# Layer boundary of a hybrid trunk: two-part dt weights, statistics in the z banks, an earlier stick-breaking chain and a fixed engine order

## The chip, the cores and the metric

One core of one Trainium2 chip. The metric is device microseconds (us) of one execution; the kernel before has a median over three runs, and one further execution was profiled.

## The reference, cut to what matters

Two post-norm residual layers over T = 272 tokens (16 learned meta tokens and 256 frames) with model width 2048. Layer 0 is four heads of gated linear attention and eight heads of stick-breaking attention behind one input and one output projection; layer 1 is a Mamba-2 mixer with 8 groups of 8 heads. After each layer comes a layer norm over `ALPHA * h + f`. All is float32.

```python
for layer in range(2):
    f = even_mixer(h, ...) if layer == 0 else odd_mixer(h, ...)
    h = layer_norm(ALPHA * h + f, ln_g[layer], ln_b[layer])

def layer_norm(x, g, b):
    xc = x - mean(x);  return xc * rsqrt(mean(xc * xc) + LN_EPS) * g + b

def odd_mixer(h, ...):
    z, xbc, dt_raw = split(h @ w_in)                # dt_raw has 64 columns
    xbc = silu(causal_conv(xbc));  xs, bs, cs = split(xbc)
    dt  = softplus(dt_raw + dt_bias)
    y   = ssd(xs, bs, cs, dt, a_log, d_skip)        # decays: exp of cumulated dt * a
    return rms_norm_groups(y * silu(z)) @ w_out
```

## The kernel before

Activations lie transposed: 16 blocks (`KT`) of 128 features by 272 tokens. Weights come from memory as "units" of 128 x 2048 f32, layer 0's units first (`L0`), then layer 1's (`L1`); tile `raw` has three buffers. Each half of a unit is split into a high and a low part (`whi` by ScalarE at L146, `wlo` mostly by VectorE at L147), each part tile with five buffers. One product is three matmuls (`three`, L165 to L167): whi by xhi, whi by xlo, wlo by xhi. An input unit is 16 blocks, so 48 matmuls into one PSUM tile `pj` (four buffers); `po` has two buffers, and two "z banks" are held apart. Side work (attention chains, convolutions, norms) are generators that `tick` steps between quarters of a unit. A list scheduler then decides the order of each engine, except where code pins it.

The place of the change is the boundary of the two layers. The last units of layer 0 are four `out0c` units (`u[2]` = 4 to 7): each adds two blocks to `hacc` (L462), after which `stat0` writes the scaled block as `xhi` (ScalarE, L815) and `xlo` (VectorE, L816), and has squares and sums for the norm gathered (ScalarE L836, GpSimd L834 and L837); the last two blocks go to TensorE unsummed (`spare`). `norm0` runs the 64 columns of the dt projection as 16 x 3 matmuls on the un-normalised blocks, then sums over features by matmuls with a matrix of ones (mean: L848, L852; squares: L849, L853), and works out mean and 1/std (L858 to L868, `newton` L253 to L255); both end in the z banks as `mean_p` and `rs_p`.

Layer 1's first six units (`NFIRST`; B, C, z and three x) also run on un-normalised blocks with two more columns, and `fix` (L899 to L902) corrects their results with mean and 1/std. Meanwhile `normalize0` centres (L927), scales (L928) and shifts (ScalarE) `hacc` block by block; then the normalised blocks are split again (`xhi` by ScalarE, `xlo` by VectorE, L920 and L921) for the seventh unit, an x unit, on. `residual1` transposes the normalised `hacc` into `acc` (L942, L943). `dt_path` makes softplus (L956 to L969) and three scans (L976), sends the sums to memory (`edr`), and transposes them on TensorE (L984, L986). `load_decay` reads `edr` back broadcast over the partitions (`ebc`), from which `decay1` makes the matrices `M` (L1047, L1048, exponential, product at L1074) that group 0's output matmuls (L1172) need.

A stick-breaking head has three units, q, k and v; `mix_sb` is its chain of scores, weights and values (values at L590), whose result `mixh` and `mixl` feed the output units.

## Time and profile before

| what | value |
|---|---|
| median of three runs | 1404.34 us (1403.64 to 1405.53) |
| the profiled execution | 1404.02 us |
| its span in the trace | 1402.3 us |
| TensorE busy | 1382.8 us, 99% of the span |
| VectorE busy | 1024.5 us, 73% |
| ScalarE busy | 769.0 us, 55% |
| GpSimd busy | 324.2 us, 23% |

The time of an execution is some 1.7 us more than the span between the first and the last instruction of the trace. Matmuls are pipelined: one of 272 columns is shown as 0.29 us long, while the next starts 0.125 us after it, so lengths of TensorE are read from start to start. A float32 matmul (not split) is recorded in two halves, so x2 stands for one of them. PE is TensorE, PEld its weight loads, DVE VectorE, ACT ScalarE, POOL GpSimd, SP the engine that issues the transfers.

### The profile page before, as it was taken

The page shows a single profiled execution, that of the slowest core. Times are in us where ns is not written, and L with a number is a line of the kernel's source. Part 1 is how long each engine was busy: PE and PEld are TensorE (multiplying, and loading weights), DVE is VectorE, ACT ScalarE, POOL GpSimd, SP SyncE. Part 2 cuts the span into 40 slices and gives each one's busy share as a digit, 9 for nine tenths or more (in the row PEclk, how much of TensorE's full clock was granted, in tenths as well). Part 3 has the DMA queues.
Part 4 walks back from the last instruction along what each step waited for, and adds up shares of the span by engine and source line. Part 5 has one row for each costly group of instructions (what it writes and reads, how often), then busy time and mean ns, then how long its engine had stood idle before and what let it go on. Part 6 is the DMA issues. An engine that isn't in the chain of part 4 may idle for free.

```text
span 1402.3 us, 26080 instructions
## 1 busy us (share of the span) xinstructions
PE 1382.8 (99%) x10701; PEld 1329.7 (95%) x10701; DVE 1024.5 (73%) x1663; ACT 769.0 (55%) x1138; POOL 324.2 (23%) x285
## 2 busy tenths in 40 slices
PE   9999999999999999999999999999999999999996
PEld 8999999999999999999999899899898999989985
DVE  7857575575565675558799989777887768778687
ACT  6645454364345544545587766555555565565651
POOL 0000110100101100114402325342332433424323
PEclk9999999999999999999999999999999999999998
DMA  9544444445444445444444755655556456454651
GB/s 326 183 153 165 168 155 176 165 167 172 159 172 160 151 154 192 156 155 142 151 151 172 265 175 192 213 192 178 207 175 227 154 192 218 161 204 149 222 196 61
DMA packets 37720, 249.84 MB, mean 178 GB/s; under 512 B 4256, under 2 KB 6112, under 8 KB 9184
## 3 DMA queue, kind: packets, MB, share of 16 engines
q1 hardware_dynamic: 37168, 247.77, 50.7%
q8 instruction: 84, 1.38, 0.4%
q10 hardware_dynamic: 432, 0.39, 0.1%
q14 instruction: 36, 0.29, 0.1%
HBM read 245.94 MB, written 2.20 MB: 177 GB/s over the span
## 4 chain that ended last, share of the span: by engine, by line
PE 83%; DVE 7%; ACT 4%; issue 2%; POOL 2%; DMA 1%; ACTq 0%; SPq 0%; POOLq 0%; DVEq 0%
PE pj L166 21%; PE pj L165 21%; PE pj L167 21%; PE pj L476 4%; PE pj L477 4%; PE pj L478 4%; DVE wlo L147 2%; PE po L1172 2%; ACT whi L146 1%; PE po L590 1%; DVE xlo L816 1%; POOL wlo L147 1%; DMA ebc<-edr 1%; DMA hacc<-in_xT 1%; POOL xt L1010 1%
## 5 line engine op out<-in xcount | busy, mean ns | idle before, releaser
L165 PE MATMUL pj<-xhi,whi 128*128 128x272 f32 (+4 forms) x2560 | 734.2, 287 | 1.5 <-ACT xhi L317 0.5
L166 PE MATMUL pj<-xlo,whi 128*128 128x272 f32 (+4 forms) x2560 | 731.3, 286 | 0.0
L167 PE MATMUL pj<-xhi,wlo 128*128 128x272 f32 (+4 forms) x2560 | 729.8, 285 | 0.0
L147 DVE TENSOR_TENSOR wlo<-raw,whi 128x1024 fp32r<-128x1024 f32 (+2 forms) x405 | 514.2, 1273 | 244.8 <-ACT whi L146 243.2
L146 ACT ACTIVATE whi<-raw 128x1024 fp32r<-128x1024 f32 (+2 forms) x435 | 451.1, 1038 | 396.4 <-PE pj L166 329.7
L165 PEld LDWEIGHTS pj<-xhi,whi 128*128 128x128 f32 x2560 | 481.6, 188 | 4.9 <-ACT whi L146 1.7
L166 PEld LDWEIGHTS pj<-xlo,whi 128*128 128x128 f32 x2560 | 482.6, 189 | 1.5 <-issue 0.6
L167 PEld LDWEIGHTS pj<-xhi,wlo 128*128 128x128 f32 x2560 | 482.0, 188 | 0.5 <-issue 0.4
L165 PE MATMUL pj<-mixh,whi 128*128 128x272 f32 x384 | 111.2, 291 | 1.0 <-ACT mixh L801 1.0
L167 PE MATMUL pj<-mixh,wlo 128*128 128x272 f32 x384 | 110.7, 289 | 0.0
L166 PE MATMUL pj<-mixl,whi 128*128 128x272 f32 x384 | 110.7, 289 | 0.0
L147 POOL TENSOR_TENSOR wlo<-raw,whi 128x1024 fp32r<-128x1024 f32 x30 | 75.7, 2524 | 118.7 <-ACT whi L146 118.5
L476 PE MATMUL pj<-whi,yh 128*128 128x512 f32 (+1 forms) x244 | 94.8, 388 | 0.0
L478 PE MATMUL pj<-whi,yl 128*128 128x512 f32 (+1 forms) x244 | 94.2, 386 | 0.0
L477 PE MATMUL pj<-wlo,yh 128*128 128x512 f32 (+1 forms) x244 | 94.2, 386 | 0.0
L248 POOL TENSOR_TENSOR gr<-gr,gsc 128x1088 f32<-128x1088 f32 x6 | 15.4, 2570 | 302.6 <-ACT gsc L247 302.6
L165 PEld LDWEIGHTS pj<-mixh,whi 128*128 128x128 f32 x384 | 72.2, 189 | 1.3 <-ACT mixh L801 1.1
L166 PEld LDWEIGHTS pj<-mixl,whi 128*128 128x128 f32 x384 | 72.3, 188 | 0.2
L167 PEld LDWEIGHTS pj<-mixh,wlo 128*128 128x128 f32 x384 | 72.3, 188 | 0.1
L485 DVE SCALAR_TENSOR_TENSOR acc<-pj,rr,acc 128x512 f32<-128x512 f32 (+1 forms) x65 | 46.1, 734 | 15.2 <-PE pj L478 15.1
L478 PEld LDWEIGHTS pj<-whi,yl 128*128 128x128 f32 x244 | 45.8, 188 | 9.2
L476 PEld LDWEIGHTS pj<-whi,yh 128*128 128x128 f32 x244 | 45.8, 188 | 9.1
(327 smaller groups left out, 1518.7 us busy)
## 6 DMA issues: line engine op xcount, KB each, us to landing
raw<-in_wts SPq DMA_DIRECT2D x212, 1024.0 KB, 4.8
ebc<-edr SPq DMA_DIRECT2D x8, 1664.0 KB, 6.4
raw<-in_wts SPq DMA_DIRECT2D x9, 256.0 KB, 5.7
hacc<-in_xT SPq DMA_DIRECT2D x7, 272.0 KB, 5.4
early<-in_wts SPq DMA_DIRECT2D x2, 512.0 KB, 7.1
lg<-in_lnr SPq DMA_DIRECT2D x1, 1024.0 KB, 4.5
lb<-in_lnr SPq DMA_DIRECT2D x1, 1024.0 KB, 4.5
out_h<-acc SPq DMA_DIRECT2D x2, 512.0 KB, 2.6
```

Source lines behind the costliest of these rows:

```text
L146: self.nc.scalar.activation(hi, src, AF.Copy)
L147: eng.tensor_tensor(lo, src, hi.bitcast(F32), op=ALU.subtract)
L165: mm(ps, whi, xhi, start=first, stop=False)
L166: mm(ps, whi, xlo, start=False, stop=False)
L167: mm(ps, wlo, xhi, start=False, stop=last)
L248: mul(c, c, e, op=ALU.mult)
L476: mm(ps, yh[:, kk, tt], hi[:, k, :], start=kk == 0, stop=False)
L477: mm(ps, yh[:, kk, tt], lo[:, k, :], start=False, stop=False)
L478: mm(ps, yl[:, kk, tt], hi[:, k, :], start=False, stop=kk == 3)
L485: self.nc.vector.scalar_tensor_tensor(a, ps, r[:, t : t + 1], a, op0=ALU.mult, op1=ALU.add)
L590: mm = lambda r, a, b, start=False, stop=False: self.nc.tensor.matmul(o[:, r], a, b, start=start, stop=stop, skip_group_check=True)
L1172: mm(o[i * 64 : (i + 1) * 64, jj, t0:S], xd[:, s, h * 64 : (h + 1) * 64], M[:, h, c0:c1], start=(s, jj) == (0, 0), stop=False, **gk,)
```

## The change

It has five parts.

1. The dt weights are loaded at `out0c` unit 4 and split at unit 5 (before: 6 and 7), with the 64 columns' high and low parts side by side in one 128-column tile. A block then takes two matmuls (both parts by xhi, both by xlo) instead of three; rows 64 to 127 of the result hold the low part's share, and one float32 matmul with `add2` (two identity matrices one above the other) adds the halves.
2. The statistics go to the z banks instead of `po` tiles, ahead of and between the dt matmuls, and that order is pinned.
3. A head's `mix_sb` starts after its k unit, one unit earlier, and waits for v only ahead of the values.
4. VectorE and ScalarE keep the order of the program from `out0c` unit 6 to the end of the centring.
5. The centring moves from `normalize0` into `norm0` and takes two blocks per instruction (128 x 544), the first two instructions ahead of `newton`; the scaling takes two blocks as well. The halves of layer 1's second unit are split there.

```diff
+    def keep_order(self, first):
+        ins = self.traced()
+        n0 = next(n for n in reversed(range(len(ins))) if ins[n] is first)
...
+        for eng in (mybir.EngineType.DVE, mybir.EngineType.Activation):
+            mine = [i for i in ins[n0:] if i.engine == eng]
+            for a, b in zip(mine, mine[1:]):
+                self.tc.add_manual_dep(b, a.name, free, reason="keep_order")
...
         if u[2] == 6:
-            self.dt_raw = self.lp.tile([P, 1024], F32, tag="gu", name="dtraw")
-            self.nc.sync.dma_start(self.dt_raw, self.wdt)
-        if u[2] == 7:
-            self.dt_parts = self.split(self.dt_raw, 1024)
+            self.first = self.traced()[-1]
+        if u[2] == 4:
+            self.dt_raw = self.lp.tile([P, 2, 8, 64], F32, tag="gu", name="dtraw")
+            self.nc.sync.dma_start(self.dt_raw.rearrange("p a k c -> p (a k c)"), self.wdt)
+        if u[2] == 5:
+            self.dt_parts = [self.lp.tile([P, 8, 2, 64], F32R, tag=n, name="dt" + n, bufs=2) for n in ("gvh", "gvl")]
+            for a, p in enumerate(self.dt_parts):
+                self.split_into(self.dt_raw[:, a], p[:, :, 0, :], p[:, :, 1, :], self.nc.vector)
...
     def post_sk(self, ps, h, j):
-        self.cur["k"] = self.sb_parts(ps, ("ke", "gk")[h % 2], 1.0)
+        k = self.sb_parts(ps, ("ke", "gk")[h % 2], 1.0)
+        v = self.cur["sv", h] = self.v_tiles(h)
+        self.mixers[4 + h // 4].append(self.push(self.mix_sb(h, self.cur["q"], k, v)))
...
-        yield from _wait(tv, self.tasks["sr", h // 4])
+        while ("sv", h) not in self.tasks:
+            yield
+        yield from _wait(self.tasks["sv", h], self.tasks["sr", h // 4])
...
-        hi, lo = [a.rearrange("p (k c) -> p k c", c=64) for a in self.dt_parts]
+        pin = self.tc.keep_in_program_order
+        pm, pq = self.zb
+        pin(mm(pm[:, :T], self.ones, self.ssum, start=True, stop=False))
+        pin(mm(pq[:, :T], self.ones, self.ssq, start=True, stop=False))
         for k in range(KT):
-            self.in_kt(self.ps_dt[:64, :TG], hi[:, k, :], lo[:, k, :], k, 0, TG)
-        pm, pq = self.po(), self.po()
...
+            if k == 10:
+                for n, (x, q) in enumerate(self.spare):
+                    l = n == len(self.spare) - 1
+                    pin(mm(pm[:, :T], self.ones, x, start=False, stop=l))
+                    pin(mm(pq[:, :T], self.ones, q, start=False, stop=l))
+            w = self.dt_parts[k // 8][:, k % 8].rearrange("p a c -> p (a c)")
+            pin(mm(self.ps_dt[:, :TG], w, self.xhi[:, k, :], start=k == 0, stop=False))
+            pin(mm(self.ps_dt[:, :TG], w, self.xlo[:, k, :], start=False, stop=k == KT - 1))
+        self.split_half(len(L0) + 1, 0)
...
+        def center(ks):
+            for k in ks:
+                h = self.hacc[:, k : k + 2, :]
+                vec.tensor_tensor(h, h, two(self.mean_p), op=ALU.subtract)
...
+        center((0, 2))
         self.newton(rs, var, tmp)
...
         act(self.rs_p, rs, AF.Copy)
+        self.split_half(len(L0) + 1, 1)
+        center(range(4, KT, 2))
+        self.keep_order(self.first)
...
-        self.tasks["dt"] = self.push(self.dt_path(fix(self.ps_dt, 64, 0, scr[:, 2048 : 2048 + T]), scr))
+        add2 = lp.tile([P, 64], F32, tag="add2", name="add2")
+        vec.tensor_tensor(add2, self.ident[:, :64], self.ident[:, 64:], op=ALU.add)
+        both = scr[:, 2048 + 2 * T : 2048 + 2 * T + TG]
+        act(both, self.ps_dt[:, :TG], AF.Copy)
+        ps = self.po()
+        nc.tensor.matmul(ps[:64, :TG], add2, both, start=True, stop=True)
+        self.tasks["dt"] = self.push(self.dt_path(fix(ps, 64, 0, scr[:, 2048 : 2048 + T]), scr))
...
-        for k in range(KT):
-            h = self.hacc[:, k, :]
-            nc.vector.tensor_tensor(h, h, self.mean_p, op=ALU.subtract)
-            nc.vector.tensor_tensor(h, h, self.rs_p, op=ALU.mult)
-            nc.scalar.activation(h, h, AF.Identity, bias=self.col(C_LB, k), scale=self.col(C_LG, k))
-            if k % 2:
-                yield
+        for k in range(0, KT, 2):
+            h = self.hacc[:, k : k + 2, :]
+            nc.vector.tensor_tensor(h, h, two(self.rs_p), op=ALU.mult)
...
```

The order of TensorE at the end of the dt projection, before (`po_8046` is the dt projection, `po_8095` the sum for the mean, `pj_8138` layer 1's first unit; the sums of squares, L849 and L853, stand 27 matmuls of `pj_8138` later):

```order
L165 MATMUL po_8046<-xhi,whi_7976 64x274
L166 MATMUL po_8046<-xlo,whi_7976 64x274
L167 MATMUL po_8046<-xhi,wlo_7977 64x274
L165 MATMUL po_8046<-xhi,whi_7976 64x274
L848 MATMUL po_8095<-ssum,ones 128x272
L852 MATMUL po_8095<-hacc,ones 128x272
L166 MATMUL po_8046<-xlo,whi_7976 64x274
L167 MATMUL po_8046<-xhi,wlo_7977 64x274
L852 MATMUL po_8095<-hacc,ones 128x272
```

And of the change (`z_64` and `z_65` are the z banks, `po_8048` the dt projection, `pj_8143` layer 1's first unit; ahead of this piece the two sums `ssum` and `ssq` go to the z banks right behind layer 0's last matmul, and then come the dt matmuls of ten blocks):

```order
L875 MATMUL po_8048<-xhi,dtgvl 128x274
L876 MATMUL po_8048<-xlo,dtgvl 128x274
L872 MATMUL z_64<-hacc,ones 128x272
L873 MATMUL z_65<-nsq_8029,ones 128x272
L872 MATMUL z_64<-hacc,ones 128x272
L178 MATMUL pj_8143<-xhi,whi_7982 128x274
L179 MATMUL pj_8143<-xlo,whi_7982 128x274
L180 MATMUL pj_8143<-xhi,wlo_7983 128x274
L178 MATMUL pj_8143<-xhi,whi_7982 128x274
L873 MATMUL z_65<-nsq_8046,ones 128x272
L875 MATMUL po_8048<-xhi,dtgvl 128x274
L876 MATMUL po_8048<-xlo,dtgvl 128x274
```

The last sum of squares now stands four matmuls of the first unit behind the sum for the mean, and the dt matmuls of the last six blocks come behind both.

The order of VectorE behind the variance, before (L253 to L255 is `newton`, L899 and L900 `fix`, L927 the centring):

```order
L860 SCALAR_TENSOR_TENSOR var<-po_8096,ntmp 128x272
L861 TENSOR_SCALAR var<-var 128x272
L253 TENSOR_TENSOR ntmp<-stats_8103 128x272
L254 SCALAR_TENSOR_TENSOR ntmp<-ntmp,var 128x272
L255 SCALAR_TENSOR_TENSOR stats_8103<-ntmp,stats_8103 128x272
L147 TENSOR_TENSOR wlo_8327<-raw_8230,whi_8326 128x1024
L880 MEMSET mt_8125 48x128
L881 MEMSET xd_8126 48x256
L899 COPY uv_8131<-po_8046 64x2
L899 COPY uv_8219<-pj_8138 128x2
L927 TENSOR_TENSOR hacc<-hacc,z_64 128x272 x11
```

And of the change (L266 to L268 is `newton`, L889 the centring, L160 the split):

```order
L894 SCALAR_TENSOR_TENSOR var<-z_65,ntmp 128x272
L895 TENSOR_SCALAR var<-var 128x272
L889 TENSOR_TENSOR hacc<-hacc,z_64 128x544 x2
L266 TENSOR_TENSOR ntmp<-stats_8091 128x272
L267 SCALAR_TENSOR_TENSOR ntmp<-ntmp,var 128x272
L268 SCALAR_TENSOR_TENSOR stats_8091<-ntmp,stats_8091 128x272
L915 MEMSET mt_8125 48x128
L916 MEMSET xd_8126 48x256
L945 TENSOR_TENSOR add_8131<-ident 128x64
L160 TENSOR_TENSOR wlo_8108<-raw_7978,whi_8107 128x1024
L889 TENSOR_TENSOR hacc<-hacc,z_64 128x544 x6
L160 TENSOR_TENSOR wlo_8219<-raw_8141,whi_8218 128x1024
```

Two centring instructions stand between the variance and `newton`, and the other six behind one split, ahead of every `fix`; before, all sixteen stood behind `newton`, eleven of them ahead of the first `fix` on the dt projection.

The order of TensorE where the dt sums are transposed, before (`pj_8990` is layer 1's tenth unit, a z unit, of which 16 matmuls stand ahead; L1061 to L1063 are scores of group 0, L984 and L986 the transposes):

```order
L165 MATMUL pj_8990<-xhi,whi_8912 128x256
L1061 MATMUL z_65<-bc_8225 128x256
L1062 MATMUL z_65<-bc_8225 128x144
L1063 MATMUL z_65<-bc_8225 16x16
L984 MATMUL po_8603<-ident,dt_scr 128x64
L166 MATMUL pj_8990<-xlo,whi_8912 128x256
L167 MATMUL pj_8990<-xhi,wlo_8913 128x256
L984 MATMUL po_8603<-ident,dt_scr 128x64 x3
L986 MATMUL po_8603<-ident,dt_scr 16x64 x2
```

And of the change (`pj_8796` is layer 1's eighth unit, `pj_8884` its ninth, both z units; L1027 and L1029 are the transposes):

```order
L179 MATMUL pj_8796<-xlo,whi_8756 128x256
L180 MATMUL pj_8796<-xhi,wlo_8757 128x256
L178 MATMUL pj_8884<-xhi,whi_8797 128x256
L1027 MATMUL po_8576<-ident,dt_scr 128x64
L179 MATMUL pj_8884<-xlo,whi_8797 128x256
L1027 MATMUL po_8576<-ident,dt_scr 128x64 x3
L1029 MATMUL po_8576<-ident,dt_scr 16x64 x2
L180 MATMUL pj_8884<-xhi,wlo_8798 128x256
```

The transposes stand behind one matmul of the ninth unit, where they stood behind sixteen of the tenth: 63 matmuls of 256 columns earlier in TensorE's order. Of the other places that TensorE waited at, the transposes of `residual1` (L942) have their fifth group of four 24 matmuls of the sixth unit behind the fourth group (before: two), the values of the last stick-breaking head stand 28 matmuls ahead of the first matmul that reads them (before: none), and group 0's output matmuls (L1172) stand behind 31 matmuls of the thirteenth unit (before: two). On SP the transfers of `edr` and `ebc` now follow the load of layer 1's twelfth unit directly; before, `edr` followed that of the thirteenth, and `ebc` that of the fourteenth.

## Rows read from the trace of the kernel before

**Rows 1.** The page: busy time, share of the span and instructions of each engine.

```profile
PE 1382.8 (99%) x10701; PEld 1329.7 (95%) x10701; DVE 1024.5 (73%) x1663; ACT 769.0 (55%) x1138; POOL 324.2 (23%) x285
```

**Rows 2.** What TensorE waited for over the whole span: line, what it waited for, us in total, times, longest.

```profile
PE po L1172 <- DVE M L1074: 1.8, 1, 1.8
PE po L942 <- ACT acc L943: 1.2, 1, 1.2
...
PE pj L165 <- ACT mixh L801: 1.0, 1, 1.0
```

**Rows 3.** TensorE in order of time around the last value matmul: start, us, instruction, in brackets the wait ahead of it and its releaser.

```profile
648.38 0.22 PE L590 MATMUL po<-s,v 80*128 80x16 f32 x1
649.60 0.77 PE L165 MATMUL pj<-mixh,whi 128*128 128x272 f32 x4 [0.99 <-ACT mixh L801]
```

**Rows 4.** TensorE in order of time through the dt projection, the statistics and layer 1's first unit (columns as in rows 3).

```profile
681.65 0.29 PE L165 MATMUL po<-xhi,whi 128*64 128x274 f32 x1
...
686.89 0.31 PE L165 MATMUL po<-xhi,whi 128*64 128x274 f32 x1
687.39 0.34 PE L166 MATMUL po<-xlo,whi 128*64 128x274 f32 x1 [0.20 <-DVE xlo L816]
...
688.54 0.34 PE L165 MATMUL po<-xhi,whi 128*64 128x274 f32 x1 [0.68 <-ACT xhi L815]
688.71 0.62 PE L848 MATMUL po<-ssum,ones 128*128 128x272 f32 x2
689.17 0.62 PE L852 MATMUL po<-hacc,ones 128*128 128x272 f32 x2
...
690.36 0.49 PE L165 MATMUL pj<-xhi,whi 128*128 128x274 f32 x1
...
698.02 0.28 PE L165 MATMUL pj<-xhi,whi 128*128 128x262 f32 x1
```

**Rows 5.** VectorE in order of time ahead of that wait.

```profile
684.69 1.21 DVE L147 TENSOR_TENSOR wlo<-raw,whi 128x1024 fp32r<-128x1024 f32 x1
685.82 0.77 DVE L462 TENSOR_TENSOR hacc<-hacc,pj 128x272 f32<-128x272 f32 x2
```

**Rows 6.** TensorE in order of time at the residual's transposes, layer 1's sixth and seventh units.

```profile
729.07 0.49 PE L942 MATMUL po<-ident,hacc 128*128 128x128 f32 x3
729.32 0.37 PE L166 MATMUL pj<-xlo,whi 128*128 128x274 f32 x1
729.53 0.29 PE L167 MATMUL pj<-xhi,wlo 128*128 128x274 f32 x1
731.05 0.66 PE L942 MATMUL po<-ident,hacc 128*128 128x128 f32 x4 [1.24 <-ACT acc L943]
732.03 0.40 PE L165 MATMUL pj<-xhi,whi 128*128 128x272 f32 x1 [0.32 <-DVE fix L900]
```

**Rows 7.** One stretch by engine: start:end and length, then busy us and instructions of PE, PEld, DVE, ACT and POOL, the granted clock, the DMA share, GB/s.

```profile
699.10:753.30 54.20, 52.64 (x433) 51.89 (x431) 54.03 (x122) 42.45 (x80) 1.43 (x1) 1.00 0.41 144
```

**Rows 8.** Groups of VectorE instructions in that stretch: count, busy us, mean ns of one, idle ahead.

```profile
L147 DVE TENSOR_TENSOR wlo<-raw,whi 128x1024 fp32r<-128x1024 f32 x16 | 19.4, 1219 | 0.2 <-ACT whi L146 0.2
...
L927 DVE TENSOR_TENSOR hacc<-hacc,z 128x272 f32<-128x272 f32 x16 | 5.7, 423 | 0.0
L928 DVE TENSOR_TENSOR hacc<-hacc,z 128x272 f32<-128x272 f32 x16 | 5.7, 423 | 0.0
```

**Rows 9.** VectorE in order of time at the beginning and the end of that stretch.

```profile
699.19 1.23 DVE L147 TENSOR_TENSOR wlo<-raw,whi 128x1024 fp32r<-128x1024 f32 x1 [0.15 <-ACT whi L146]
...
700.83 3.90 DVE L927 TENSOR_TENSOR hacc<-hacc,z 128x272 f32<-128x272 f32 x11
...
751.42 0.42 DVE L901 TENSOR_TENSOR fix<-fix,z 128x272 f32<-128x272 f32 x1
751.77 0.48 DVE L999 SCALAR_TENSOR_TENSOR xt<-fix,cpk,xt 128x269 f32<-128x269 f32 x1
752.18 1.14 DVE L976 TENSOR_TENSOR_SCAN dt_scr<-dt_scr 64x272 f32<-64x272 f32 x3
```

**Rows 10.** TensorE in order of time: the first matmul of the eighth unit, and the first transpose of the dt sums.

```profile
739.42 0.28 PE L165 MATMUL pj<-xhi,whi 128*128 128x256 f32 x1
...
753.04 0.27 PE L984 MATMUL po<-ident,dt_scr 64*128 64x64 f32 x1
```

**Rows 11.** The chain that ended last, between the scans and M: start, us, what.

```profile
752.81 0.52 DVE dt_scr L976 x2
...
753.34 2.10 DMA edr<-dt_scr
...
755.51 9.28 DMA ebc<-edr
```

**Rows 12.** TensorE in order of time at group 0's output.

```profile
770.78 0.28 PE L166 MATMUL pj<-xlo,whi 128*128 128x272 f32 x1
772.91 0.65 PE L1172 MATMUL po<-M,xd 128*64 128x256 f32 x4 [1.85 <-DVE M L1074]
```

**Rows 13.** VectorE in order of time, early in layer 0: instructions of 544 columns.

```profile
39.70 3.90 DVE L385 SCALAR_TENSOR_TENSOR hacc<-hacc,shiftc 128x544 f32<-128x544 f32 x6
```

**Rows 14.** ScalarE in order of time: the mean, and the copy of 1/std to its z bank.

```profile
691.13 0.38 ACT L858 ACTIVATE stats<-po 128x272 f32<-128x272 f32 x1
...
699.07 0.40 ACT L868 ACTIVATE z<-stats 128x272 f32<-128x272 f32 x1
```

**Rows 15.** GpSimd in order of time: one addition of squares while VectorE splits weights, and one while it doesn't.

```profile
659.56 1.75 POOL L837 TENSOR_TENSOR ssq<-ssq,nsq 128x272 f32<-128x272 f32 x1
...
681.99 0.77 POOL L837 TENSOR_TENSOR ssq<-ssq,nsq 128x272 f32<-128x272 f32 x1
```

**Rows 16.** The page: the loads of units; count, KB each, median us from issue to landing.

```profile
raw<-in_wts SPq DMA_DIRECT2D x212, 1024.0 KB, 4.8
```

More of the change, by code (lines that the diff above doesn't have):

```diff
@@ L149, in split_half @@
     def split_half(self, i, h):
-        if i < NU:
+        if i < NU and (i, h) not in self.parts:
             n = i - len(L0)
@@ L857, in norm0 @@
         tmp = lp.tile([P, T], F32, tag="ge", name="ntmp")
+        self.mean_p, self.rs_p = [z[:, :T] for z in self.zb]
+        two = lambda a: a.rearrange("p (o t) -> p o t", o=1).broadcast_to([P, 2, T])
+        def center(ks):
+            for k in ks:
+                h = self.hacc[:, k : k + 2, :]
+                vec.tensor_tensor(h, h, two(self.mean_p), op=ALU.subtract)
         act(mean, pm[:, :T], AF.Copy, scale=1.0 / D)
         act(tmp, mean, AF.Square)
+        act(self.mean_p, mean, AF.Copy)
         vec.scalar_tensor_tensor(var, pq[:, :T], 1.0 / D, tmp, op0=ALU.mult, op1=ALU.subtract)
@@ L863, in norm0 @@
         act(rs, rs, AF.Exp, scale=-0.5)
+        center((0, 2))
         self.newton(rs, var, tmp)
-        self.mean_p, self.rs_p = [z[:, :T] for z in self.zb]
-        act(self.mean_p, mean, AF.Copy)
         act(self.rs_p, rs, AF.Copy)
+        self.split_half(len(L0) + 1, 1)
+        center(range(4, KT, 2))
+        self.keep_order(self.first)
     def layer1(self):
@@ L924, in normalize0 @@
         nc = self.nc
-        for k in range(KT):
-            h = self.hacc[:, k, :]
-            nc.vector.tensor_tensor(h, h, self.mean_p, op=ALU.subtract)
-            nc.vector.tensor_tensor(h, h, self.rs_p, op=ALU.mult)
-            nc.scalar.activation(h, h, AF.Identity, bias=self.col(C_LB, k), scale=self.col(C_LG, k))
-            if k % 2:
-                yield
+        two = lambda a: a.rearrange("p (o t) -> p o t", o=1).broadcast_to([P, 2, T])
+        for k in range(0, KT, 2):
+            h = self.hacc[:, k : k + 2, :]
+            nc.vector.tensor_tensor(h, h, two(self.rs_p), op=ALU.mult)
+            for kk in (k, k + 1):
+                a = self.hacc[:, kk, :]
+                nc.scalar.activation(a, a, AF.Identity, bias=self.col(C_LB, kk), scale=self.col(C_LG, kk))
+            yield
     def residual1(self, norm):
```

15 lines of the change are left out of this document (5 added, 10 removed).

## The prediction

> **What bounds the kernel now.** The page's first part says TensorE: it is busy 99% of the span, no other engine over 73% [rows 1]. So the time is TensorE's work plus its waits, and only what shortens one of these counts. I read next what TensorE waits for: three waits stand at this change's places, 1.8 us for `M`, 1.2 for `acc` and 1.0 for `mixh` [rows 2]. Then I read TensorE in order of time at each of them, start to start.
>
> At the first, the 16-column value matmul starts at 648.38 and the next at 649.60 [rows 3]. I count the 0.99 in brackets and a little of the rest: 1.1 us.
>
> At the second place, the boundary, I call 681.65 T0: the first dt matmul. The forty-third starts at 686.89, so a dt matmul takes 5.24 / 42 = 0.125 us. Then come waits for `xlo` and `xhi`, and layer 1's first unit starts only at 690.36, its second at 698.02, T0 + 16.37 [rows 4]. The late thing is `hacc`: VectorE splits a weight at 684.69, and only at 685.82 adds layer 0's last two blocks [rows 5], though their last matmul starts just ahead of T0.
>
> At the third, a matmul starts at 729.53, the transposes at 731.05 and the next unit at 732.03 [rows 6]. Without waits the first step would take 0.125, and four transposes 0.34 (three took 0.25 there, 729.07 to 729.32). So 1.40 + 0.64 = 2.0 us are lost.
>
> At the fourth, 770.78 to 772.91 holds one matmul of 0.125 and a wait of 2.0 us [rows 12].
>
> The last thing to see is VectorE. From 699.10 to 753.30 it is busy 54.03 of 54.20 us [rows 7], and the dt scans stand at the end of that stretch [rows 9]. TensorE's transposes of their result start at 753.04, behind the first scan, which ends by 752.81 [rows 10, 11]. So VectorE, 73% busy on average, is full here, and what TensorE gains at the boundary it keeps only if VectorE reaches the scans earlier too.
>
> **The change part by part.** I make the sum against the profiled execution's 1404.02 us; the median of 1404.34 lies 0.3 above it, and I add that at the end.
>
> *Stick-breaking chain from k on.* The values now stand 28 matmuls ahead of their first reader, 28 x 0.125 = 3.5 us, against a wait of 1.1. It goes: **-1.1**. The chain's earlier work lies beside a unit of projections; if it collided there, at most this 1.1 would be lost.
>
> *TensorE at the boundary.* The change has 32 dt matmuls x 0.125 = 4.0; six statistics matmuls at 0.46 (688.71 to 689.17 in [rows 4]) = 2.76; 48 of the first unit at 0.127 = 6.08; in all 12.84. The fixed order puts both additions to `hacc` ahead of the splits, and ten blocks of dt and three statistics stand ahead of the last blocks' `xhi` and `xlo`, so I take no wait. The matmul with `add2` is float32 with 272 columns, another 0.46. That makes 13.30 against 16.37: **-3.07**. The dt split that moves earlier has a whole unit (6 us) of room, so I cost it at nothing; the `ScalarE` copy of the dt sums (about 0.4, like the copies in [rows 14]) lies beside TensorE's second unit.
>
> *Residual's transposes.* With 24 matmuls between the fourth and fifth group (24 x 0.125 = 3.0 us) the copy to `acc` and the last `fix` are in time: **-2.0**.
>
> *VectorE's chain to the scans.* Before, `rs_p` is written at 699.07 [rows 14], and from 699.19 to 752.81 the chain takes 53.62 us. Now:
> - sixteen centrings at 0.35 (eleven in 3.90 us [rows 9]) leave: -5.6. Eight instructions of 544 columns come, two ahead of `newton`, six in the chain. Six of 544 took 3.90 us elsewhere [rows 13], and their starts are 0.64 apart: +3.84.
> - scaling: sixteen at the same price [rows 8] become eight of 0.64: -0.45.
> - the order has one more split ahead of the first scan, 1.15 (1.219 with its overlap [rows 8]), seven conv steps fewer at 0.41 (751.77 to 752.18 [rows 9]): -2.87, one pair of `fix` fewer, 0.41 + 0.35: -0.76, and the `add2` addition: +0.2.
>
> The sum is 53.62 - 5.6 + 3.84 - 0.45 + 1.15 - 2.87 - 0.76 + 0.2 = 49.1 us. No row shows a 544-wide instruction with its second operand in a z bank, stretched over two blocks. From below it costs 0.64, as from SBUF; from above, two of 272, 0.70; I take 0.64, since one of 272 from a z bank costs no more than its neighbours. An end far above is a rival below.
>
> [...]
>
> The chain's start: the mean is complete after two statistics, twenty dt matmuls and three statistics, T0 + 4.8, the squares four matmuls and 0.46 later, T0 + 5.8. Then a copy and two VectorE steps, logarithm and exponential (0.4 each, beside which two centrings lie) and three steps of `newton` end at T0 + 9.6 to 10.1. Before it was T0 + 17.5. So the first scan is done at T0 + 58.7 to 59.2 if VectorE never waits. It may: each split needs a `whi` from ScalarE in one of five buffers that TensorE must free, and VectorE now runs some 4 us further ahead of TensorE. I bound that idle time by 0 and 2.5.
>
> *TensorE against that chain.* TensorE comes to the transposes after one matmul of the ninth unit. Before, it was there at 739.42 + 48 x 0.1125 + 0.11 = 744.93, T0 + 63.3 [rows 10]. Less 3.07 and 2.0 that is T0 + 58.2. The scan isn't done then; it ends between T0 + 58.7 and 61.7, so a new wait of 0.5 to 3.5 us takes back part. I take 1.5: **+1.5**, with TensorE past it at about T0 + 59.8.
>
> *`M`.* The chain behind the scans, 2.10 for `edr` and 9.28 for `ebc` [rows 11], then `M` on VectorE, ended before at about 772.8 [rows 12], 19.7 behind the transposes' start. TensorE used to be there 17.9 behind it. Now the transposes stand 63 matmuls of 256 columns earlier and the reader 29 of 272 later: 17.9 + 7.1 + 3.6 = 28.6 against 19.7. The wait goes, with 9 us to spare: **-2.0**. What is moved past on SP is the thirteenth unit's load: it lands 4.8 us after its issue [rows 16], waits for `edr` till about T0 + 62, and its first matmul is due near T0 + 83. I cost it at nothing; without that cover it would be 2.1 us, `edr`'s transfer.
>
> Sum: -1.1 - 3.07 - 2.0 + 1.5 - 2.0 = -6.7, or 1397.3 against 1404.02; with the 0.3 to the median, **1397.6**.
>
> **The rivals.** *R1, VectorE gives nothing:* idle for part buffers, or an order that holds a split of ScalarE ahead of the dt `fix`, makes the scans end at T0 + 63 still. Then the 5.07 of boundary and transposes turn into a wait at the transposes, and only the values' wait and that for `M` go: 1404.3 - 3.1 = 1401.2. For it speaks that VectorE has no idle time to lose [rows 7]; against it, 4.5 us less of work and a start 7.5 us earlier.
>
> *R2, sums late.* The pinned sums of `ssum` and `ssq` stand first, and everything on TensorE behind them. GpSimd makes an addition in 0.77 alone, 1.75 beside a split [rows 15]. The thirteenth and fourteenth blocks are ready some 6 us ahead of T0; four additions at 1.75 make 7.0, so TensorE and the chain behind it would start 1.3 late: 1398.9. Against it: VectorE splits only 2.3 us of those 6. [...]
>
> *R3, slower: the two-wide instruction is dear.* Sixteen of them lie on the chain that leads to the scans. Each 0.1 us above 0.64 costs 1.6 us. At 1.06 the whole 6.7 is gone; from 1.23 the kernel is slower by over 0.2%; at 1.25 it is 16 x 0.61 = 9.8 later, or 1407.4. For it: no row shows this operand. Against it: the rows of 272 with a z bank.
>
> **How the numbers follow.** Chances: forecast 0.70, R1 0.15, R2 0.08, R3 0.07. The forecast's own range goes from 1395.2 (no wait at the transposes would be -8.2; and VectorE's better end gives up to 0.9 more) to 1399.6 (a wait of 3.5). With R1 the range reaches 1401.5; that leaves out R3 and some of the ends. The measured runs spread over 0.13%, so 0.2%, 2.8 us, is about what can be told from no change. The forecast and R2 are faster, R1 lies at -0.22%, so I share it between faster and same, and R3 goes mostly to slower: 0.85, 0.10, 0.05.
>
> **What would show it.** In the changed kernel's trace the second unit of layer 1 should start about T0 + 13 (the `add2` matmul lies in that unit), VectorE's first centring about T0 + 7, a 544-wide one take 0.64, and the dt scans come near T0 + 59, with a wait of 0.5 to 3.5 us at the transposes behind them. No wait should stand at the values, the fifth transposes, or group 0's output. I am wrong if VectorE shows idle time of more than 2.5 us between the centring and the scans, if TensorE waits at the seventh unit for the normalised `xlo`, which VectorE writes in the same chain, or if a wait moves into the stick-breaking units.

## The result, and the profile after

The changed kernel takes 1408.36 us, median of ten runs (1406.28 to 1409.36), the kernel before 1404.81 in ten (1403.64 to 1407.20). The ratio is 1.0020, with an interval of 1.0012 to 1.0029. That is slower by 0.2%, where I had forecast 1397.6 and a range up to 1401.5. The profiled execution took 1409.36 us, 5.34 more than that of before. It is as slow as the slowest of the ten, so what is worked out below from the two traces is for 5.34 us and not for the 3.55 between the medians.

The page of the changed kernel, busy time and share of each engine, as [rows 1]:

```profile
PE 1384.7 (98%) x10687; PEld 1331.6 (95%) x10687; DVE 1023.0 (73%) x1649; ACT 769.4 (55%) x1140; POOL 323.5 (23%) x285
```

VectorE, ScalarE and GpSimd have no more work than before; TensorE is on record for 1.9 us more with fourteen instructions fewer, which the clock will explain. What TensorE waited for, as [rows 2] (line, awaited, us in total, times, longest):

```profile
PE po L1154 <- POOL xt L1053: 6.2, 2, 6.0
PE pj L178 <- DVE fix L935: 2.0, 1, 2.0
...
PE po L985 <- ACT acc L986: 0.3, 1, 0.3
```

The waits for `mixh` and `M` are gone, that for `acc` has shrunk. In their place stand two that no step of the prediction names: 6.0 us at the transposes of `xt` (L1154), whose data GpSimd makes, and 2.0 us at the first matmul of layer 1's eighth unit, whose PSUM buffer `fix` of the fourth unit must first read.

TensorE of the changed kernel in order of time, at the boundary, at the eighth unit, at the dt transposes and at the transposes of `xt` (start, us, instruction, wait ahead of it):

```profile
680.14 0.62 PE L866 MATMUL z<-ssum,ones 128*128 128x272 f32 x2
681.22 0.73 PE L867 MATMUL z<-ssq,ones 128*128 128x272 f32 x2 [0.46 <-POOL ssq L857]
...
693.75 0.28 PE L178 MATMUL pj<-xhi,whi 128*128 128x262 f32 x1
...
734.69 0.28 PE L180 MATMUL pj<-xhi,wlo 128*128 128x272 f32 x1
736.95 0.38 PE L178 MATMUL pj<-xhi,whi 128*128 128x256 f32 x1 [1.97 <-DVE fix L935]
...
742.92 0.27 PE L1027 MATMUL po<-ident,dt_scr 64*128 64x64 f32 x1
...
760.77 0.28 PE L180 MATMUL pj<-xhi,wlo 128*128 128x272 f32 x1
767.07 1.12 PE L1154 MATMUL po<-ident,xt 128*128 128x128 f32 x4 [6.02 <-POOL xt L1053]
```

The reader is to see that the dt transposes now start at 742.92. Before, TensorE came to the same point at 744.93, so of the 4.6 us that I expected to have won by here less than half is left. The loss comes 18 us later: from 760.77 to 767.07 TensorE does one matmul of 0.125, so 6.2 us are lost.

GpSimd of the changed kernel around that wait:

```profile
755.23 1.51 POOL L249 TENSOR_SCALAR_AFFINE_SELECT cb<-cb 128x112 f32<-128x112 f32 x3 [8.61 <-DVE M L1091]
758.90 8.11 POOL L1053 TENSOR_TENSOR xt<-xt,xcl 128x544 f32<-128x544 f32 x1 [2.16 <-ACT xcl L1052]
```

One multiplication of 544 columns is on record for 8.11 us. The same one in the kernel before:

```profile
758.10 2.07 POOL L1010 TENSOR_TENSOR xt<-xt,xcl 128x544 f32<-128x544 f32 x1 [0.23 <-ACT xcl L1009]
```

VectorE of the changed kernel in the same stretch:

```profile
757.84 1.21 DVE L160 TENSOR_TENSOR wlo<-raw,whi 128x1024 fp32r<-128x1024 f32 x1
758.97 1.87 DVE L1117 TENSOR_TENSOR M<-M,cb 128x800 f32<-128x800 f32 x2
760.78 0.21 DVE L1098 TENSOR_SCALAR mt<-mt 16x128 f32<-16x128 f32 x1
760.91 0.48 DVE L1042 SCALAR_TENSOR_TENSOR xt<-fix,cpk,xt 128x269 f32<-128x269 f32 x1
761.32 1.21 DVE L160 TENSOR_TENSOR wlo<-raw,whi 128x1024 fp32r<-128x1024 f32 x1
762.46 1.88 DVE L1117 TENSOR_TENSOR M<-M,cb 128x800 f32<-128x800 f32 x2
764.26 1.20 DVE L160 TENSOR_TENSOR wlo<-raw,whi 128x1024 fp32r<-128x1024 f32 x1
765.40 0.42 DVE L1049 TENSOR_SCALAR xcl<-xt 128x544 f32<-128x544 f32 x1
```

From 757.84 to 765.82 VectorE goes without a gap from one instruction with operands in SBUF to the next, and the multiplication ends at 767.01, 1.2 us behind the end of this run; less the 1.35 that one takes where nothing holds it, it begins at 765.66, within the last of them. In this run stand the four products of `M` (L1117), 3.6 us, which the kernel before had only from 771.79 on, since its `ebc` landed only at 764.8 [rows 11]. The change brought `M` forward by 12 us: as forecast it is no longer waited for, but it now stands ahead of what TensorE needs first.

The same stretch and what follows, by engine, as [rows 7] (busy us and instructions of PE, PEld, DVE, ACT, POOL; granted clock; DMA share; GB/s):

```profile
760.70:767.10 6.40, 0.38 (x4) 0.17 (x3) 5.17 (x9) 1.35 (x3) 6.31 (x1) 0.92 0.85 316
767.10:770.00 2.90, 2.90 (x14) 2.75 (x14) 2.74 (x8) 0.00 (x0) 0.00 (x0) 0.50 0.02 8
770.00:773.00 3.00, 3.00 (x15) 3.00 (x15) 1.45 (x2) 2.54 (x5) 0.00 (x0) 0.51 0.88 311
773.00:776.00 3.00, 3.00 (x27) 3.00 (x26) 0.76 (x3) 2.79 (x5) 0.00 (x0) 1.00 0.10 41
```

Behind the wait the granted clock stands at 0.50 to 0.51 for some 6 us: 29 matmuls in 5.9 us where the last row does 27 in 3.0 (0.111 each). That costs another 5.9 - 29 x 0.111 = 2.7 us.

So the balance is: 2.0 won up to the dt transposes, 2.0 at `M`, 6.2 lost to the wait at `xt` and 2.7 to the clock behind it, +4.9 of the +5.34 measured. The other 0.4 I have not placed.

### The profile page after: what moved, and what is told of

Its sections match the earlier page's. It is cut to its first block, busy times and chain, and to the rows that moved or that the text cites. A ratio compares the mean times of both kernels' runs of the same rounds, so it can differ in the third digit from the quotient of the medians.

```text
span 1407.6 us, 26031 instructions
## 1 busy us (share of the span) xinstructions
PE 1384.7 (98%) x10687; PEld 1331.6 (95%) x10687; DVE 1023.0 (73%) x1649; ACT 769.4 (55%) x1140; POOL 323.5 (23%) x285
## 5 line engine op out<-in xcount | busy, mean ns | idle before, releaser
L160 DVE TENSOR_TENSOR wlo<-raw,whi 128x1024 fp32r<-128x1024 f32 (+2 forms) x405 | 513.5, 1271 | 265.8 <-ACT whi L159 264.2
L160 POOL TENSOR_TENSOR wlo<-raw,whi 128x1024 fp32r<-128x1024 f32 x30 | 75.4, 2512 | 119.3 <-ACT whi L159 119.1
```

The source lines that it names most:

```text
L160: eng.tensor_tensor(lo, src, hi.bitcast(F32), op=ALU.subtract)
```

## The experiments

The theory after the result was: **A**, VectorE's run keeps GpSimd's multiplication out, and the products of `M` in it are what the change added. Rivals: **A1**, GpSimd's instruction is merely slow there, or starts at an unlucky moment, whatever VectorE does; **B**, `xt` is late by its own chain on ScalarE, or its transposes stand too early on TensorE; **C**, the transfers that land meanwhile (DMA share 0.85) slow GpSimd; and that the loss lies in part 1, 3 or 4 of the change and not at `xt`. Ratios are to the kernel before as measured beside each run, with medians of 1404.96 to 1405.59.

Nearly every edit makes the scheduler order the engines anew. So I say where the transposes of `xt` stand on TensorE: in the changed kernel behind 183 matmuls of units, counted from the first of the eighth.

**The products of `M` behind `xt`.** Of the changed kernel, group 0's decay is made to wait for the task of `xt`, and the first product ordered behind the first multiplication by dt:

```
+        if g == 0:
+            yield from _wait(self.tasks["x", 0, 3])
...
+            if (g, h) == (0, 0):
+                self.tc.add_manual_dep(self.traced()[-1], self.xd_first.name, free, reason="M behind x")
```

> The changed kernel, with one thing moved: group 0's products of M by the scores (VectorE, two inputs in SBUF) are held on VectorE behind its first multiplication of the transposed x; GpSimd's multiplication of x, the transposes' place on TensorE and all else stay. Theory A: in the changed kernel TensorE waits 6.0 us at the x transposes because GpSimd's multiplication can't get at its operands while VectorE runs two-input instructions (M products and splits) back to back; after the wait the granted clock is half for some 5 us, which costs another 2.6. A expects: the GpSimd multiplication ends within 2.1 us of its start, the wait at the transposes falls below 0.5 us, the clock stays at 1.00, and the time is about 1409.4 - 6.2 - 2.6 = 1400.6 us (1399 to 1402), 0.3% faster than the kernel before. Rival B: x itself is late (its chain of exponentials on ScalarE ends only at 758.8), or the transposes merely stand too early on TensorE; then the wait stays at 4 to 6 us and the time at 1407 to 1409. Rival C: the transfers (DMA share 0.85 in that wait) slow GpSimd; then it stays at 6 as well, since they are not moved.

Measured: 1404.71 us (1403.45 to 1406.35), ratio 1.0001 (0.9991 to 1.0010). That is outside A's 1399 to 1402, but the edit did a part of what it was meant to: only one of the four products moved (to 768.43), three still ran ahead. GpSimd and VectorE of this kernel:

```profile
758.42 6.08 POOL L1053 TENSOR_TENSOR xt<-xt,xcl 128x544 f32<-128x544 f32 x1 [2.15 <-ACT xcl L1052]
```

```profile
761.08 1.87 DVE L1119 TENSOR_TENSOR M<-M,cb 128x800 f32<-128x800 f32 x2
762.88 0.42 DVE L1049 TENSOR_SCALAR xcl<-xt 128x544 f32<-128x544 f32 x1
```

The run has a product and a split less, 2.0 us, and all lies 0.5 earlier here; it ends at 763.30 instead of 765.82, and the multiplication ends 2.5 earlier too, at 764.50. TensorE waits 3.0 there instead of 6.0, with the transposes still behind 183 matmuls. So with all four moved:

```
-            if (g, h) == (0, 0):
+            if g == 0:
```

> As the run with M behind x, but all four products of group 0 are held behind the first multiplication of the transposed x (there three of the four still ran ahead of it, and the wait was 3.0 us). By theory A the run of two-input instructions ahead of GpSimd's multiplication is shorter by three products of 0.9 us and the split between, so the wait at the x transposes is 0 to 1 us, the clock stays up, and the time is 1400 to 1402 us. If x's own chain or the transfers were the cause, the wait stays at 3 us and the time at 1404.7.

Measured: 1401.38 (1400.73 to 1401.84), ratio 0.9972 (0.9960 to 0.9983), within A's range and 7.0 us below the changed kernel. GpSimd of this kernel, and the end of VectorE's run:

```profile
758.16 3.37 POOL L1053 TENSOR_TENSOR xt<-xt,xcl 128x544 f32<-128x544 f32 x1 [2.16 <-ACT xcl L1052]
...
766.47 9.59 POOL L1053 TENSOR_TENSOR gz<-gz,xcl 128x512 f32<-128x512 f32 x2 [0.37 <-ACT xcl L1052]
```

```profile
759.91 0.42 DVE L1049 TENSOR_SCALAR xcl<-xt 128x544 f32<-128x544 f32 x1
```

The multiplication of `xt` is kept out only until the shorter run ends at 760.33, and TensorE's wait there falls to 1.0. The transposes still stand behind 183 matmuls, so B is out: five of the 6.0 us went without a later place. The products, now from 766.84 on, meet the next multiplication, that of `gz`, and hold that one, together with the instructions behind them, for 7.1 us (8.35 for the first of the two against 1.28 alone). The DMA share is 0.32 in that stretch (766.5 to 774.8) and 0.91 where the multiplication of `xt` took 3.37, so C is out too. Products alone are not what it takes: at `xt` the run without any still kept GpSimd out for 2.0 us, from 758.16 to about 760.2. They made the run long enough to matter.

**The multiplication of `xt` on VectorE.**

```
-        self.nc.gpsimd.tensor_tensor(v, v, c, op=ALU.mult)
+        (eng or self.nc.gpsimd).tensor_tensor(v, v, c, op=ALU.mult)
...
+        eng = vec if (g, j) == (0, 0) else None
```

> The changed kernel, but group 0's first multiplication of x (128x544, behind the exponentials) runs on VectorE instead of GpSimd; the scheduler then puts the first x transposes 28 matmuls later on TensorE. Theory A (GpSimd kept from its operands by VectorE's two-input instructions) expects no wait over 0.5 us at these transposes, full clock, and 1399 to 1402 us. Rival B (x's chain on ScalarE is late by itself): the multiplication starts late too, the wait shrinks only by the 3.5 us of the later place, to 2 to 3 us, and the time is 1403 to 1406.

Measured: 1400.27 (1399.85 to 1400.43), ratio 0.9961 (0.9946 to 0.9975), 8.1 us below the changed kernel and as expected. No wait is left at the transposes:

```profile
764.80 0.60 PE L1155 MATMUL po<-ident,xt 128*128 128x128 f32 x4
```

But the 8.1 us are not the price of that one instruction. VectorE multiplies at 763.05, also only when its turn comes, for 0.71 us; that is 3.3 us sooner than GpSimd was done. The rest of the wait goes because the scheduler put the transposes 28 matmuls later, behind 211. At their old place, 761.40 here, TensorE would still have waited 2.4. The wait of 2.0 at the eighth unit stays, and in this kernel the clock falls behind it (the same columns as above):

```profile
736.40:740.00 3.60, 3.55 (x17) 3.55 (x18) 3.60 (x9) 0.64 (x2) 0.00 (x0) 0.53 0.78 280
740.00:743.60 3.60, 3.60 (x33) 3.60 (x33) 3.60 (x11) 3.60 (x7) 0.07 (x1) 1.00 0.12 32
```

17 matmuls where the next 3.6 us hold 33: 1.7 us lost. In the changed kernel itself the wait at this place is as long and the clock stays at 1.00, so the profile of this kernel has a loss that the other doesn't have.

**The price by itself.** Two kernels with nothing but GpSimd's multiplication and runs of VectorE's instructions; in the second, runs of splits, of products and of the kernel's mixture, each in fixed order and with a release at fourteen moments:

> Not the reference's computation: a kernel of its own that measures one thing, GpSimd's multiplication of two 128x544 tiles, released at the same moment as a run of VectorE instructions, eight cases, twice each: no VectorE work; 6 splits (128x1024, two inputs in SBUF); 7 products (128x800, two in SBUF); 11 centrings (128x544, one input in SBUF and one in PSUM); 22 of one input (128x544); 17 conv steps (128x272, two in SBUF); 2 splits; 12 splits. Theory A expects some 1.4 us alone and beside centrings and one-input instructions, and beside splits, products and conv steps an end only behind VectorE's whole run: about 8 us at 6 splits, 3.7 at 2, 15 at 12. Rival D (the engines take turns instruction by instruction): no more than one VectorE instruction is waited for, at most 2.7 us in each case, whatever the length of the run.

> Not the reference's computation: a kernel of its own. VectorE runs back to back, in fixed order: 8 splits; or 10 products of 800 columns; or a mixture as in the changed kernel (split, two products, conv step, split, two products, split); each run closed by a one-input instruction. GpSimd's multiplication of 128x544 (1.4 us alone) is released by a ScalarE copy whose length is stepped by some 0.08 us, 14 steps for each run. Theory A1 (what the earlier rows suggest): released while an instruction of two SBUF inputs is under way, GpSimd gets its turn at that instruction's end, 1.4 to 2.6 us in all; released in the last 0.1 us of one, it misses that turn and all later ones, and ends only behind the run, 5 to 9 us in all; 1 or 2 of 14 offsets. Rival D (a fair turn at each boundary): never more than about 2.6 us. Rival A (kept out by every such run): always till the run's end.

Measured: 1.33 to 2.18 us in the first kernel, the shortest where VectorE's instruction reads PSUM, and never above 2.42 in the 42 stages of the second, down to 1.33. The first kernel didn't test what it was meant to: the scheduler mixed the kinds of instructions, and in seven of its sixteen stages GpSimd was released beside the last one ahead of a wait for it. The second has the order fixed. GpSimd of the second, the longest:

```profile
117.78 2.42 POOL L68 TENSOR_TENSOR v<-v,w 128x544 f32<-128x544 f32 x1 [10.92 <-ACT w L67]
```

GpSimd waits 2.42 - 1.33 = 1.1 us here, less than one split takes (1.21 in the first kernel). In the first kernel it gets its turn at the next boundary between two VectorE instructions, and VectorE's next one waits instead: a product took 2.11 us (from 16.75 on), 0.98 otherwise. So neither the kind of instruction nor the moment of release, as tried here, makes 8 us. The theories that had long stages in them missed, and rival D, a turn at the next boundary, came true in both: A1's unlucky moment isn't found, and A in the plain form "a run of VectorE's instructions keeps GpSimd out" isn't reproduced either. The next two runs went back to the kernel.

**A later release.** A ScalarE copy of 16 columns, then one of 400, stands ahead of GpSimd's multiplication:

```
+        if late:
+            act(c[:, :late], c[:, :late], AF.Copy)
```

> The changed kernel, x still on GpSimd, VectorE's order unchanged up to behind group 0's products of M; one more ScalarE copy of 16 columns (some 0.2 us) stands between x's exponentials and GpSimd's multiplication of x, so that it is released 0.2 us later against VectorE's run of two-input instructions; the scheduler puts the first x transposes 19 matmuls (2.4 us) later. Theory A2 (the moment of release decides: in the changed kernel it falls 0.07 us ahead of the next instruction of VectorE, behind which GpSimd then finds no turn; released well inside one it gets the next turn): the multiplication takes at most 2.6 us instead of 8.1, no wait above 0.5 us, 1400 to 1402 us. Theory A (kept out as long as VectorE runs two-input instructions, whenever released): it still ends some 8 us later, TensorE waits 6.0 - 2.4 = 3.6 us, and the time is about 1405.

> As before it, with the extra copy 400 columns wide (some 0.5 us), so that GpSimd is released 0.3 us later still. A2: at most 2.6 us for the multiplication again, unless the release falls just ahead of a start once more (then several us). A: about 7.5 us.

Measured: 1405.16 (1403.51 to 1406.27), ratio 0.9997 (0.9987 to 1.0006), and 1405.12 for the second, in a single execution. GpSimd of the first, and the end of VectorE's run:

```profile
760.69 6.04 POOL L1055 TENSOR_TENSOR xt<-xt,xcl 128x544 f32<-128x544 f32 x1 [4.24 <-ACT xcl L1054]
```

```profile
765.11 0.42 DVE L1049 TENSOR_SCALAR xcl<-xt 128x544 f32<-128x544 f32 x1
```

Released 1.8 us later (in the second 2.2, at 761.06, for 5.72 us), the multiplication ends at 766.73 (766.78), where it ended at 767.01. Its end doesn't hang on its start but on VectorE's run, which ends at 765.53 in the first of these (and 765.82 in the changed kernel). In both of these, in the changed kernel and in the two with products moved, it ends 1.2 us behind the end of the same instruction of VectorE (L1049). So A holds in the kernel, and a slow instruction is out. That these kernels are 3 us faster than the changed one has to do with TensorE's order: the transposes stand 18 and 21 matmuls later, and TensorE waits 2.6 and 4.0. The first waits less, since it came there later: its granted clock was 0.84 from 734 to 745, where the wait at the eighth unit lies, that of the second 1.00.

**Which ingredient.** The isolated run once more, with the order of the kernel and, in turn, what it lacked: instructions that don't wait for one another, inputs from ScalarE, loads, busy engines:

> This kernel doesn't compute the reference: it measures one cost by itself. GpSimd's 544-wide multiplication is released, by a ScalarE copy of four lengths, into a run of VectorE instructions with two inputs (split, 2 products of M, one fix, split, 2 products, split: about 12 us), behind which stands one instruction with one input. Six cases of four stages each: nothing else; VectorE's instructions writing the same tile each time, so that each waits for the one before it; the inputs made by ScalarE just ahead; loads landing; ScalarE and TensorE busy; and the last three together. Theory S (it was the wait of each VectorE instruction for the one before it that gave GpSimd its turn in the two isolated kernels): without such waits the multiplication takes 5 to 11 us and ends only behind the run, with them at most 2.6. Theory I (one of the other ingredients keeps GpSimd out): only the stages with that ingredient are long. Theory N (none of these): at most 2.6 us in all twenty-four stages, and what keeps it out in the kernel stays open.

Measured: 1.48 to 2.20 us in all twenty-four stages. GpSimd in the longest, which has all ingredients:

```profile
231.17 2.20 POOL L67 TENSOR_TENSOR v<-v,w 128x544 f32<-128x544 f32 x1 [9.47 <-ACT w L66]
```

That is theory N. None of these ingredients, as tried here, keeps GpSimd out, and why it gets no turn at nine boundaries in a row in the kernel stays open.

**The stick-breaking chain undone.** The kernel with `xt` on VectorE, and part 3 of the change taken back:

```
-        k = self.sb_parts(ps, ("ke", "gk")[h % 2], 1.0)
-        v = self.cur["sv", h] = self.v_tiles(h)
-        self.mixers[4 + h // 4].append(self.push(self.mix_sb(h, self.cur["q"], k, v)))
+        self.cur["k"] = self.sb_parts(ps, ("ke", "gk")[h % 2], 1.0)
...
+        self.mixers[4 + h // 4].append(self.push(self.mix_sb(h, self.cur["q"], self.cur["k"], v)))
```

> The kernel with x on VectorE (1400.3 us), but the stick-breaking chain starts after the v unit again, as before. The forecast's step: the wait of 1.1 us ahead of the last output units comes back at the values, all behind it moves by as much: 1401.4 to 1401.8. Rival: VectorE paces TensorE between the norm and the transposes of the dt sums, and its part isn't later, so the wait there shrinks by the same: 1400.3.

Measured: 1401.94 (1400.28 to 1403.18), by the medians 1.67 us more than with it, a little over the expected 1.1 to 1.5; the ranges of the two kernels touch. TensorE's wait is back:

```profile
PE pj L178 <- ACT mixh L821: 1.0, 1, 1.0
```

TensorE comes to layer 1's eighth unit 1.6 us later (738.07 instead of 736.45), behind the same wait of 2.0 for `fix`. So VectorE is later by as much, and the rival is out. Behind that place the orders differ (the dt transposes stand behind 75 matmuls instead of 49), so the 1.67 as a whole is not shown to be this wait's.

**The dt projection in three matmuls of 64 columns.** The kernel with `xt` on VectorE; the weights side by side are used one after the other, so that `add2`, the copy `both` and the matmul with it fall away, and the last statistics stand behind 21 dt matmuls instead of 20. TensorE gets 48 dt matmuls again instead of 32:

```
-            if k == 10:
+            if k == 7:
...
+            w, d = self.dt_parts[k // 8], self.ps_dt[:64, :TG]
+            pin(mm(d, w[:, k % 8, 0], self.xhi[:, k, :], start=k == 0, stop=False))
+            pin(mm(d, w[:, k % 8, 0], self.xlo[:, k, :], start=False, stop=False))
+            pin(mm(d, w[:, k % 8, 1], self.xhi[:, k, :], start=False, stop=k == KT - 1))
...
-        act(both, self.ps_dt[:, :TG], AF.Copy)
-        ps = self.po()
-        nc.tensor.matmul(ps[:64, :TG], add2, both, start=True, stop=True)
```

> The kernel with x on VectorE, but the dt projection takes three matmuls of 64 columns for a block again, without the one with add2; the last statistics stand behind 21 dt matmuls instead of 20, so that the mean comes as early as before. TensorE has 16 x 0.125 - 0.46 = 1.54 us more to do. If VectorE paces TensorE up to the ninth unit (wait of 2.0 us for a fix at the eighth), the wait shrinks by that and the time stays within 0.5 us of 1400.3. If TensorE's own work counts, 1401.8.

Measured: 1397.31 (1396.73 to 1397.53), ratio 0.9939 (0.9925 to 0.9954): the fastest of all, 2.96 us below the kernel with `add2`, though TensorE has 16 x 0.125 - 0.7 = 1.3 us more to do (the matmul with `add2` took 0.7). Neither of the two expected times, 1400.3 and 1401.8, came. VectorE of the kernel with `add2` (`xt` on VectorE), at the dt sums and at the fourth unit's `fix`:

```profile
702.19 0.48 DVE L935 SCALAR_TENSOR_TENSOR dt_scr<-dt_scr,uv,po 64x272 f32<-64x272 f32 x1
...
704.15 1.23 DVE L160 TENSOR_TENSOR wlo<-raw,whi 128x1024 fp32r<-128x1024 f32 x1 [1.07 <-ACT whi L159]
...
735.91 0.48 DVE L935 SCALAR_TENSOR_TENSOR fix<-dt_scr,uv,pj 128x272 f32<-128x272 f32 x1
```

And of the kernel with three matmuls:

```profile
700.12 0.48 DVE L936 SCALAR_TENSOR_TENSOR dt_scr<-dt_scr,uv,po 64x272 f32<-64x272 f32 x1
...
733.35 0.48 DVE L936 SCALAR_TENSOR_TENSOR fix<-dt_scr,uv,pj 128x272 f32<-128x272 f32 x1
```

With `add2` the dt sums are there only behind half a unit of TensorE; VectorE's order has five splits between the centring and the first dt `fix`, without it three, and the dt sums come 2.07 us later on VectorE. Full but for a few gaps, VectorE carries the delay on, and the `fix` that frees the eighth unit's buffer comes at 735.91 instead of 733.35. TensorE needs that buffer at about 734.3. So the wait of 2.0, the one at L985 and the half clock behind the first, 2.1 + 0.4 + 1.7 = 4.2 us, go, and 1.3 of work come: 2.9 of the 2.96. The sum leaves out that the order changed elsewhere too (the transposes of `xt` stand behind 234 matmuls instead of 211).

**That alone, with `xt` on GpSimd as in the changed kernel.**

```
-        eng = vec if (g, j) == (0, 0) else None
+        eng = None
```

> The changed kernel itself with the dt projection in three matmuls of 64 columns again (last statistics behind 21 of them, no add2), x on GpSimd as in the change. In the run with x on VectorE this part took the wait of 2.0 us for a fix away, with the half clock behind it, and made 3 us. If its effect is there only through VectorE's order between the norm and the scans, the same 3 us come here on top of whatever GpSimd's multiplication costs: 1405.4 if it still takes 8 us (1408.4 - 3), 1396 to 1398 if the collision is gone because the places shift.

Measured: 1399.51 (1399.01 to 1400.09), ratio 0.9957 (0.9941 to 0.9974), between the two expectations of 1405.4 and 1396 to 1398. GpSimd of this kernel:

```profile
757.77 3.86 POOL L1048 TENSOR_TENSOR xt<-xt,xcl 128x544 f32<-128x544 f32 x1 [19.77 <-ACT xcl L1047]
761.59 0.67 POOL L249 TENSOR_SCALAR_AFFINE_SELECT cb<-cb 128x112 f32<-128x112 f32 x3
```

Here the selection on `cb` stands behind the multiplication of `xt` on GpSimd, not ahead of it as in the changed kernel. The products of `M` need `cb`, so they can't get into the run. The multiplication is still kept out for 2.5 us and ends at 761.63, and TensorE doesn't wait for it, since its transposes stand 37 matmuls later than in the changed kernel, at 761.98; at the old place, 757.5 here, it would have waited 4.1. A new wait of 1.6 us for GpSimd's `ysq` stands at 803.84. The four kernels make a table:

| | `xt` on GpSimd | `xt` on VectorE |
|---|---|---|
| dt in two matmuls and `add2` | 1408.36 (the change) | 1400.27 |
| dt in three matmuls | 1399.51 | 1397.31 |

Either edit turns the change from slower than before to faster; the second of them then adds 2.2 or 3.0. These are prices of an edit together with what the scheduler makes of it. The price of the collision with TensorE's order as it was is the 7.0 us of the run with all products moved.

## Why the prediction was wrong, step by step

**The step that failed** is the one on `M`. "The wait goes, with 9 us to spare" was right: no wait for `M` is left. But I read the 12 us by which `M` comes earlier as nothing but room, and asked only who waits for `M`. I didn't ask beside what its products would now be done. They land on VectorE just as GpSimd is to make `xt`, and TensorE waits for that: 6.2 us and 2.7 of half clock behind it, where the sum had nothing. A row for the question was shown: GpSimd's additions took 0.77 alone and 1.75 beside a split [rows 15]. I priced that contention for `ssq` only. Even so the price would have been too small: a turn in rows 15 costs 1.0, in the isolated kernels it cost at most 1.1, and here it was 6.75, over nine boundaries between VectorE's instructions. R2 named a contention of the same two engines, at another place and at 1.3 us in all.

**Part 1, -3.07 at the boundary, gave -2.1.** From the first statistic T0' at 680.14 to the second unit there are 13.61 us (I had 12.84 without `add2`). The first two statistics take 1.44 of them, up to the first dt matmul at 681.58, instead of 0.92: 0.5 us is the wait for the sum of squares, so R2 came true in a small part. The matmul with `add2` took 0.7 instead of 0.46; 16.37 - 13.61 - 0.7 is 2.1.

**"I cost it at nothing"** for the copy of the dt sums was wrong. The copy lies beside TensorE's second unit, as I said; but the dt `fix` on VectorE waits for the matmul behind it, and all that stands behind on VectorE with it. That is the 2.1 us wait at the eighth unit; with the wait at L985 and the clock, where it fell, it is 4.2 us. The prediction bounded VectorE's idle time between 1/std and the scans by 2.5 us; in the changed kernel it is 2.25 (0.84 at 691.81, 1.07 at 704.66, 0.34 at 718.10).

**The new wait at the dt transposes, +1.5, did not come.** VectorE's scans of the changed kernel:

```profile
741.54 1.14 DVE L1019 TENSOR_TENSOR_SCAN dt_scr<-dt_scr 64x272 f32<-64x272 f32 x3
```

The second starts at 742.17, so the first is done by T0' + 62.0, just past the late end of my 58.7 to 61.7. TensorE came to the transposes no sooner than that, since it had already waited at the eighth unit. The wait was foreseen in size (2.1 instead of 1.5) and set 6 us too late: the lateness of VectorE met TensorE at an earlier point. That the sizes are near is luck: without `add2` (the run with three dt matmuls and `xt` on VectorE) the wait at the eighth unit is gone and the first scan still ends only at T0' + 62.4.

**Right were:** the values' wait (forecast -1.1; T0' is 1.5 earlier than T0, and with the part undone the wait of 1.0 was back); the residual's transposes, -1.6 of -2.0; the wait for `M`, -2.0; the 544-wide centring. The centring of the changed kernel:

```profile
692.95 3.87 DVE L889 TENSOR_TENSOR hacc<-hacc,z 128x544 f32<-128x544 f32 x6
```

Six in 3.87 is 0.645 each, so R3 is out.

**The chances** were wrong because all the rivals priced the chain that I had followed. "Slower" rested on one dear instruction with 0.07; that a chain which becomes earlier collides with another engine's work had no chance at all. No run shows the 0.9 us by which "VectorE's better end" lowers the range to 1395.2: the two-wide instruction took the 0.645 that the sum had, and the first scan was done by T0' + 62.0, later than the 58.7 to 61.7 that I gave it.

## What to carry to other kernels

When a chain moves forward, list what each of its instructions will then stand beside, not only who waits for its end: here 3.6 us of products, 12 us earlier, cost 8.9 us of TensorE's time in the trace, and 7.0 came back when they were moved. An edit that saves matmuls but adds a copy and a further step ahead of a full engine is to be priced on that engine's path. Where a scheduler orders the engines, look in each run for what else moved before a difference is put down to the edit. And where TensorE is the bound, a wait's price is its length plus that of the half clock where one follows: here 6.2 and 2.7 us.

## What the runs showed of the hardware that I had not expected

- GpSimd's multiplication of 544 columns, 1.33 to 1.37 us where nothing held it, was kept out for 6.75 us by nine VectorE instructions behind one another in the changed kernel, and one of 512 for 7.1 us with the products moved. A run of two splits, a conv step and a short instruction kept it out for 2.0. In three isolated kernels with instructions of the same kinds, 16, 42 and 24 stages, it never waited over 1.1. Later in the changed kernel, too, it got its turn at the first boundary, and VectorE's second split waited (two splits, 3.52 us from 1046.63 on, 2.35 where they don't). GpSimd there:

```profile
1046.77 2.30 POOL L1053 TENSOR_TENSOR xt<-xt,xcl 128x544 f32<-128x544 f32 x1 [3.92 <-DVE xt L1042]
```

  What makes the difference is not settled. Landing transfers alone are not it: the four stages with loads and nothing else in the last isolated kernel took 1.81 to 2.15.
- After the wait of 6.0 us TensorE's granted clock was at 0.50 for 5.9 us. After the one of 2.0 at the eighth unit it was 0.53 from 736.40 to 740.00 with `xt` on VectorE, and 0.84 from 734 to 745 with the copy of 16 columns; with the copy of 400 it was 1.00 in that stretch, and in the changed kernel 1.00 from 736.90 to 743.00. After the wait of 2.6, with the copy of 16 columns, it stayed at 1.00 (760 to 775).
